# Attention in a hybrid trunk layer: the prompt's probabilities transposed by DMA instead of TensorE

## The chip, the cores and the metric

The kernel runs on one core of a Trainium2 chip. The metric is device time in microseconds of one execution. TensorE multiplies matrices and writes to PSUM; VectorE (DVE), ScalarE (ACT) and GpSimd (POOL) work on SBUF, and the first two also on PSUM; SyncE (SP) issues most transfers. Each engine, and each queue of transfers, works through its own instructions in a fixed order, and waits on semaphores where an instruction needs another engine's result.

## The reference

One layer serves 1024 prompt tokens and 8 sample requests of 16 tokens with the same weights. After a modulated norm one wide projection gives the attention's q, k, v and gate, the inputs of a state-space (SSD) branch, and two merge gates. The attention is banded: a chunk of 64 tokens sees itself and the 8 chunks before it, with a bias by distance.

```python
def attend(q, k, v, bias, mask):
    s = jnp.einsum('bqhd,bkhd->bhqk', q, k).astype(jnp.float32) * (ATT_HEAD_DIM ** -0.5) + bias[None].astype(jnp.float32)
    s = jnp.where(mask, s, -1e30)
    p = jax.nn.softmax(s, axis=-1).astype(v.dtype)
    return jnp.einsum('bhqk,bkhd->bqhd', p, v)

q = rms_norm(q.reshape(b, s, ATT_HEADS, ATT_HEAD_DIM), q_norm_g)
k = rms_norm(k.reshape(b, s, ATT_HEADS, ATT_HEAD_DIM), k_norm_g)
o_att, k_st, v_st = attn_fn(q, k, v)
att_branch = (o_att.reshape(b, s, ATT_WIDTH) * jax.nn.silu(z_att)) @ w_att_proj
```

There are 16 heads of 64. The SSD branch, the two projections back, the gates and the output projection follow; the outputs also hold the last k and v rows and the states. The change touches the attention alone. All values are float32.

## The kernel before, in words

Tokens: 1024 prompt and 128 sample tokens, 1152 (`NT`) in all, nine tiles of 128. A large product is made of three matmuls in a reduced float32 form, high part by high part, high by low and low by high, so weights and operands are split in two (L334, L335).

**Units.** The attention is done in eight units of two heads (`attention(u)`, L910). A unit has four parts, written as Python generators:

- `dense_gen` (L915): `dense_tok` (L487) makes q, k and v of the unit for nine token tiles, 24 matmuls a tile (L506 to L508), each into one of two PSUM banks "d"; after a tile `ev` (L923) copies q and k to the buffer `qk` (L926) with their squares (L928) on ACT and v on DVE (L929, L932). `dense` (L427; matmuls L442, L443, L445) then makes the next unit's gate columns z.
- `prelude` (L945): in three parts (first four tiles, next four, the sample tokens' tile) it norms q and k on POOL (L955 to L958), transposes them on TensorE (L980, for the sample tokens L990) and splits them into the operands `qh, ql, kh, kl` of the scores. There is one set of these; the set of unit u comes free when the last scores of unit u are done. Part one also takes places for the keys to be stored (`ko`) and the two heads' biases.
- `prompt` (L1037): the scores, softmax and weighing of the prompt, in six rounds.
- `sample` (L1141): the same for the sample requests against the cache, in two halves, with ten transposes of its own by the helper `transposed`.

**A prompt row block.** For query block m (128 tokens) a head has n = min(m,4)+1 blocks of 128 keys. The scores (L1101) go to PSUM; DVE adds the bias, negates and takes the row's least value (`negated`, L1024); ACT exponentiates with a row sum (`exps`, L1019), DVE scales by the reciprocal (L1020, L1021). The n blocks of probabilities are transposed on TensorE (`transposed`, L1031), copied from PSUM back into the same place by ACT (first four, L1033) and DVE (the fifth, L1035), and weighed with v on TensorE (`weigh`, L1054); DVE multiplies the result by the gate (L1106).

**Places.** Score rows lie in SBUF places "S" of 640 columns, nine of them; a place holds one head's row of a block. Blocks 0 and 3 share a pair of places, and 1 and 2. `ko` and the two biases also lie in "S" places.

**Rounds.** `ROUNDS` (L1065) lists, for each round, the score pieces, the blocks then weighed, and the blocks then transposed.

**What sets the order.** `run` (L841) plays a small planner. It steps the dense generator, adds the TensorE cost that each step yields to a clock, and gives the same times a ratio (0.95 here) as credit to "paced" generators (`prompt`, `sample`); "urgent" ones (`prelude`, stores) go first whenever they can. Waits are written as due times on that clock (`until`, `pause`), for instance:

```python
sfree[0] = clock[0] + 300 + sum(3.2 * x[2] for x in pieces)
tpt[m] = clock[0] + 1100
```

`sfree` is the time from which the next round, or the sample's scores, may use the score banks "s"; `tpt[m]` the time from which block m may be weighed. The order of the calls is the order that a scheduler below starts from: it may move an instruction forward where its operands are ready sooner, except for those under `late`, which stay behind the instruction before them on their engine. SP's queue carries the loads of weights (L312), of the cache (L1154, L1179) and of biases (L971, L1150), and the stores of k, v and the attention result (L1000, L937, L1013).

## Time and profile before

| | us |
|---|---|
| median of 3 runs (1954.15 to 1954.44) | 1954.2 |
| the profiled execution | 1954.12 |
| its span, first to last instruction | 1952.4 |
| TensorE busy | 1938.9 |
| DVE / ACT / POOL busy | 1163.5 / 775.9 / 328.1 |
| attention's transposes L1031, first and last start | 111.8 and 736.7 |

In the rows below a line number is a line of the kernel, "PE" is TensorE and "PEld" its weight loads. The page's first part gives each engine's busy time, share of the span and instructions; the chain of work follows the last instruction back to what released it. A row of a group has line, engine, operation, tile written and read, shapes, count, then busy us and the mean ns of one, then the idle time before it and what ended it. A window row has the stretch, its length, then busy time and count of each engine asked for (PE, PEld, DVE, ACT, POOL), the granted clock, the DMA engines' busy share and GB/s. A timeline row has start, duration, engine, line, operation, tiles, shapes and count. A matmul's duration overlaps the next one's, so the cost of one is the distance between starts.

### The profile page before, as it was taken

What the parts mean: (1) busy time and instruction counts of PE and PEld (TensorE: products, weight loads), DVE (VectorE), ACT (ScalarE), POOL (GpSimd) and SP (SyncE); (2) the same over time, 40 slices, a digit from 0 to 9 for tenths busy, and PEclk for the clock granted to TensorE, in tenths of its full rate; (3) what the DMA queues carried; (4) which work ended last, traced back from release to release, by engine and by line L of the source; (5) the groups of instructions that cost most, each with busy time, mean ns of one, the idle gap of its engine ahead of it and who ended that gap; (6) DMA issues with size and microseconds to landing.
All of it is one profiled execution on the core that took longest, in us unless ns stands there. A gap on an engine that the chain in (4) does not pass through costs nothing.

```text
span 1952.4 us, 34857 instructions
## 1 busy us (share of the span) xinstructions
PE 1938.9 (99%) x14041; PEld 1856.1 (95%) x14041; DVE 1163.5 (60%) x2409; ACT 775.9 (40%) x1579; POOL 328.1 (17%) x624
## 2 busy tenths in 40 slices
PE   8999999999999999999999999999999999999999
PEld 5989999899998899999999999999999999999999
DVE  7455545555455766666666766666674334777732
ACT  8444444444444565344434434345351301111200
POOL 0312223122221201211221221122212100000000
PEclk9999999999999999999999999999999999999999
DMA  9223343233332443334233333332337642331241
GB/s 374 63 70 122 103 138 118 72 119 109 131 111 71 133 125 119 129 117 131 92 127 119 116 105 106 117 118 91 118 119 292 232 140 92 105 104 56 86 143 53
DMA packets 81208, 238.61 MB, mean 122 GB/s; under 512 B 14284, under 2 KB 15320, under 8 KB 81048
## 3 DMA queue, kind: packets, MB, share of 16 engines
q1 hardware_dynamic: 72088, 207.74, 32.4%
q0 software_dynamic: 8960, 28.65, 3.8%
q8 instruction: 110, 1.80, 0.4%
q14 instruction: 50, 0.41, 0.1%
HBM read 192.70 MB, written 43.66 MB: 121 GB/s over the span
## 4 chain that ended last, share of the span: by engine, by line
PE 98%; ACT 0%; DVE 0%; DMA 0%; issue 0%; SPq 0%; DVEq 0%; ACTq 0%
PE d L442 14%; PE d L443 14%; PE d L445 14%; PE s L442 6%; PE s L445 6%; PE s L443 6%; PE d L508 5%; PE d L506 5%; PE d L507 5%; PE g L1031 3%; PE g L1054 3%; PE g L1542 2%; PE s L1101 2%; PE g L1515 1%; PE g L1562 1%; PE g L1101 1%
## 5 line engine op out<-in xcount | busy, mean ns | idle before, releaser
L442 PE MATMUL d<-rarena 128*128 128x384 f32 x1520 | 515.8, 339 | 0.0
L443 PE MATMUL d<-rarena 128*128 128x384 f32 x1520 | 511.3, 336 | 0.0
L445 PE MATMUL d<-rarena 128*128 128x384 f32 x1520 | 511.0, 336 | 0.0
L443 PEld LDWEIGHTS d<-rarena 128*128 128x128 f32 x1520 | 285.6, 188 | 2.8 <-issue 2.6
L442 PEld LDWEIGHTS d<-rarena 128*128 128x128 f32 x1520 | 285.7, 188 | 2.3 <-issue 0.9
L445 PEld LDWEIGHTS d<-rarena 128*128 128x128 f32 x1520 | 285.9, 188 | 0.4 <-issue 0.4
L334 ACT ACTIVATE rarena<-arena 128x1024 fp32r<-128x1024 f32 x92 | 97.4, 1059 | 330.9 <-PE s L443 238.3
L442 PE MATMUL s<-rarena 128*128 128x384 f32 x640 | 216.8, 339 | 0.0
L445 PE MATMUL s<-rarena 128*128 128x384 f32 x640 | 214.3, 335 | 0.0
L443 PE MATMUL s<-rarena 128*128 128x384 f32 x640 | 214.1, 334 | 0.0
L506 PE MATMUL d<-va_att,rarena 128*128 128x384 f32 (+1 forms) x559 | 194.1, 348 | 0.0
L508 PE MATMUL d<-va_att,rarena 128*128 128x384 f32 (+1 forms) x559 | 193.1, 345 | 0.0
L507 PE MATMUL d<-va_att,rarena 128*128 128x384 f32 (+1 forms) x559 | 190.2, 341 | 0.0
L335 DVE TENSOR_TENSOR rarena<-arena,rarena 128x1024 fp32r<-128x1024 f32 x92 | 113.2, 1231 | 81.8 <-ACT rarena L334 81.4
L1019 ACT ACTIVATE arena<-arena 128x640 f32<-128x640 f32 (+3 forms) x144 | 101.3, 706 | 70.6 <-DVE arena L1119 40.5
L442 PEld LDWEIGHTS s<-rarena 128*128 128x128 f32 x640 | 120.3, 188 | 1.1 <-issue 1.0
L443 PEld LDWEIGHTS s<-rarena 128*128 128x128 f32 x640 | 120.3, 188 | 0.0
L445 PEld LDWEIGHTS s<-rarena 128*128 128x128 f32 x640 | 120.2, 188 | 0.0
L1033 ACT ACTIVATE arena<-g 128x512 f32<-128x512 f32 (+3 forms) x144 | 71.3, 523 | 106.2 <-PE g L1031 106.0
L508 PEld LDWEIGHTS d<-va_att,rarena 128*128 128x128 f32 x559 | 105.2, 188 | 3.6 <-issue 3.2
L506 PEld LDWEIGHTS d<-va_att,rarena 128*128 128x128 f32 x559 | 105.6, 189 | 2.7 <-issue 1.9
L507 PEld LDWEIGHTS d<-va_att,rarena 128*128 128x128 f32 x559 | 105.3, 188 | 0.5 <-DVE arena L643 0.4
(345 smaller groups left out, 3224.1 us busy)
## 6 DMA issues: line engine op xcount, KB each, us to landing
arena<-in_wall_dram SPq DMA_DIRECT2D x85, 512.0 KB
arena<-in_kc_dram SPq DMA_DIRECT2D x64, 256.0 KB
arena<-in_vc_dram SPq DMA_DIRECT2D x64, 256.0 KB
arena<-acs_d SPq DMA_DIRECT2D x20, 576.0 KB
gate_d<-arena POOLq DMA_DIRECT2D x48, 192.0 KB, 2.8
arena<-y_d SPq DMA_DIRECT2D x15, 576.0 KB
arena<-in_wssd_dram SPq DMA_DIRECT2D x16, 512.0 KB
arena<-eacs_d SPq DMA_DIRECT2D x28, 288.0 KB
```

The lines of the kernel that those rows point to most:

```text
L334: keep(nc.scalar.activation(hi.r[:, c], b.ap, AF.Copy))
L335: keep(nc.vector.tensor_tensor(lo.r[:, c], b.ap, hi.ap[:, c], ALU.subtract))
L442: nc.tensor.matmul(ps, hi.r[:, wc], kh.r[:, tok], start=k == 0, stop=False)
L443: nc.tensor.matmul(ps, hi.r[:, wc], kl.r[:, tok], start=False, stop=False)
L445: nc.tensor.matmul(ps, lo.r[:, wc], kh.r[:, tok], start=False, stop=k == nk - 1)
L506: nc.tensor.matmul(ps, kh.r[:, tok], wh, start=j == 0, stop=False)
L507: nc.tensor.matmul(ps, kh.r[:, tok], wl, start=False, stop=False)
L508: nc.tensor.matmul(ps, kl.r[:, tok], wh, start=False, stop=j == KT - 1)
L1019: nc.scalar.activation(p, p, AF.Exp, bias=sm_[:, 4 + e:5 + e], scale=-1.0, accum_out=sm_[:, 6 + e:7 + e])
L1031: nc.tensor.transpose(ps[:, s * P:(s + 1) * P], p[:, (j + s) * P:(j + s + 1) * P], ident)
L1033: nc.scalar.activation(pt[:, j * P:(j + n) * P], ps[:, :n * P], AF.Copy)
L1054: late(nc.tensor.matmul(po[e * HD:e * HD + HD, a * P:(a + 1) * P], v.ap[:, vc:vc + HD], x.ap[:, o + i * P:o + (i + 1) * P], start=i == 0, ...
```

## The change

The prompt's probabilities are no longer transposed on TensorE. After the softmax, `turn(m)` runs for block m, as an urgent generator, for both heads:

1. It takes a second pair of places (`turned`), shared by blocks 0 and 3 and by 1 and 2 as before.
2. ACT copies the row from its place to the new one, taken as 16-bit words, so that all low halves of the float32 words come first and all high halves after (`words` to `planes`).
3. A transfer on SP's queue transposes the 2n blocks of 128x128 half-words from there back into the old place.
4. Due 7.5 us after the probabilities, ACT (head 1) and DVE (head 0) put the halves together again as words in the new place, from which `weigh` reads.
5. The old pair of places is freed then, and the block may be weighed 4.5 us later.

The third column of `ROUNDS` and the transposes in the round loop are gone; a round now also waits until its blocks have a due time, and takes places in pairs, only when no block still waits for its second pair. The due time of the score banks gets longer.

To make room for a tenth "S" place, `qk` has 16 blocks instead of 18, so that the ninth token tile lies where the first lay, and its eviction waits in `ev` until the first tokens are transposed; there is one "d" place (the sample's query block) instead of two and one "p" instead of two; the sample's own keys get a place "k" of their own, so that `ko` can be freed after its store; "t" has six places instead of five.

```diff
-    L_ATT = arena.set_layout(Z0, [("Q", 1, 18 * P), ("T", 5, NT), ("S", 9, 640), ("U", 2, 640), ("K", 4, 512), ("q", 1, 256), ("d", 2, 256),
-                                  ("p", 2, 128), ("n", 2, 36 + 3 * 16), ("t", 5, 14)])
+    L_ATT = arena.set_layout(Z0, [("Q", 1, 16 * P), ("T", 5, NT), ("S", 10, 640), ("U", 2, 640), ("K", 4, 512), ("q", 1, 256), ("d", 1, 256),
+                                  ("k", 1, 128), ("p", 1, 128), ("n", 2, 36 + 3 * 16), ("t", 6, 14)])
...
             def ev(t, ps):
-                c = qk.ap[:, 2 * t * P:2 * (t + 1) * P]
+                while t == 8 and "turned" not in st:
+                    blocked[0] = "q and k of the first tokens"
+                    yield None
+                c = qk.ap[:, 2 * (t % 8) * P:2 * (t % 8 + 1) * P]
...
+                    st["turned"] = True
                 else:
+                    ks = yield from walloc(lay, "k", P)
+                    qd = yield from walloc(lay, "d", 256)
+                    late(nc.gpsimd.memset(qd.ap, 0.0))
+                    yield from pause(600)
...
                     nc.scalar.activation(ko.ap[:, 512:], ps[:, P:], AF.Copy, scale=par["qk_g"][:, 1:2])
+                    nc.scalar.activation(ks.ap, ps[:, P:], AF.Copy, scale=par["qk_g"][:, 1:2])
                     yield 218
                     yield from pause(900)
                     dma(h["out_k"][u], ko.ap)
+                    stored(ko)
...
+            pairs = {0: 3, 1: 2, 2: 1, 3: 0}
+            def planes(x, at, n):
+                return x.ap[:, at:at + n * P].bitcast(U16).rearrange("p (t k) -> p t k", t=2)
+            def words(x, at, n):
+                return x.ap[:, at:at + n * P].bitcast(U16).rearrange("p (k t) -> p t k", t=2)
+            def turn(m):
+                n = min(m, 4) + 1
+                if pairs.get(m) in claimed:
+                    yield from ready(lambda: m in turned)
+                else:
+                    claimed.add(m)
+                    t = yield from wpair(lay, "S", 640)
+                    for q, at in ((m, place[m][0][1]), (pairs.get(m), {0: 4 * P, 2: 2 * P}.get(pairs.get(m), 0))):
+                        if q is not None:
+                            turned[q] = [(b, at) for b in t]
+                turning[0] -= 1
+                for e in range(2):
+                    yield from until(probs[m] + 800 * e)
+                    (x, at), (y, _) = place[m][e], turned[m][e]
+                    nc.scalar.activation(planes(y, at, n), words(x, at, n), AF.Copy)
+                    dma(x.ap[:, at:at + n * P].bitcast(U16).rearrange("p (i k) -> p i k", k=P),
+                        y.ap[:, at:at + n * P].bitcast(U16), transpose=True)
+                for e in range(2):
+                    yield from until(probs[m] + 800 * e + 7500)
+                    (x, at), (y, _) = place[m][e], turned[m][e]
+                    if e:
+                        nc.scalar.activation(words(y, at, n), planes(x, at, n), AF.Copy)
+                    else:
+                        nc.vector.tensor_copy(words(y, at, n), planes(x, at, n))
+                xs = place.pop(m)
+                if pairs.get(m) not in place:
+                    for x, _ in xs:
+                        x.free()
+                tpt[m] = clock[0] + 4500
...
             ROUNDS = (
-                (((0, 0, 128, 0, 0), (1, 0, 256, 0, 128), (2, 0, 384, 1, 0)), (), ()),
-                (((3, 0, 512, 0, 0), (4, 0, 512, 1, 0)), (), (0, 1, 2)),
-                (((4, 512, 128, 0, 0), (5, 0, 320, 0, 128), (5, 320, 320, 1, 0)), (0, 1, 2), (3,)),
-                (((6, 0, 320, 0, 0), (6, 320, 320, 1, 0)), (3,), (4, 5)),
-                (((7, 0, 320, 0, 0), (7, 320, 320, 1, 0)), (4, 5), (6, 7)),
-                ((), (6, 7), ()),
+                (((0, 0, 128, 0, 0), (1, 0, 256, 0, 128), (2, 0, 384, 1, 0)), ()),
+                (((3, 0, 512, 0, 0), (4, 0, 512, 1, 0)), ()),
+                (((4, 512, 128, 0, 0), (5, 0, 320, 0, 128), (5, 320, 320, 1, 0)), (0, 1, 2)),
+                (((6, 0, 320, 0, 0), (6, 320, 320, 1, 0)), (3,)),
+                (((7, 0, 320, 0, 0), (7, 320, 320, 1, 0)), (4, 5)),
+                ((), (6, 7)),
             )
...
-                        if m in (2, 3):
-                            place[m] = [(x, at) for x, _ in place[3 - m]]
-                        else:
-                            place[m] = []
-                            for e in range(2):
-                                place[m].append(((yield from walloc(lay, "S", 640)), at))
+                        t = yield from wpair(lay, "S", 640, lambda: turning[0] == 0)
+                        for q in {m, pairs.get(m, m)}:
+                            place[q] = [(x, {0: 4 * P, 2: 2 * P}.get(q, 0)) for x in t]
...
+                        turning[0] += 1
+                        urgent.append(turn(m))
...
-                sfree[0] = clock[0] + 300 + sum(3.2 * x[2] for x in pieces)
-                for m in ts:
-                    n = min(m, 4) + 1
-                    yield from until(sfree[0])
-                    for e in range(2):
-                        yield from until(probs[m] + 700 * e)
-                        x, at = place[m][e]
-                        transposed(x.ap[:, at:at + n * P], x.ap[:, at:at + n * P], n)
-                        yield 109 * n
-                    tpt[m] = clock[0] + 1100
-                    sfree[0] = max(sfree[0], clock[0] + 1500)
+                sfree[0] = clock[0] + 1000 + sum(4.4 * x[2] for x in pieces)
```

More of the change, by code (lines that the diff above doesn't have):

```diff
@@ L266, in walloc, with wpair @@
                 yield None
+    def wpair(lay, tag, cols, cond=lambda: True):
+        while True:
+            try:
+                if cond():
+                    a = alloc(lay, tag, cols)
+                    try:
+                        return [a, alloc(lay, tag, cols)]
+                    except NoSlot:
+                        a.free()
+                        raise
+                blocked[0] = "places for what is transposed"
+            except NoSlot as x:
+                blocked[0] = str(x)
+            yield None
     x0_ = Z0
@@ L1057, in weigh @@
                 for j in js:
-                    for x, _ in place.pop(j):
-                        if not any(x is y for q in place.values() for y, _ in q):
+                    for x, _ in turned.pop(j):
+                        if pairs.get(j) not in turned:
                             x.free()
@@ L1065, in prompt @@
             ROUNDS = (
[6 rows of a table removed]
-            )
-            for pieces, js, ts in ROUNDS:
[6 rows of a table added]
+            )
+            for pieces, js in ROUNDS:
+                yield from ready(lambda: all(j in tpt for j in js))
                 yield from until(max([sfree[0]] + [tpt[j] for j in js]))
```

34 lines of the change are left out of this document (18 added, 16 removed).

## The prediction, made before the changed kernel was run

> **What bounds the kernel now.** I read the page's busy shares first, then the chain that ended last, then the windows of one attention unit, then that unit's timeline engine by engine. From the page:
>
> ```profile
> PE 1938.9 (99%) x14041; PEld 1856.1 (95%) x14041; DVE 1163.5 (60%) x2409; ACT 775.9 (40%) x1579; POOL 328.1 (17%) x624
> PE 98%; ACT 0%; DVE 0%; DMA 0%; issue 0%; SPq 0%; DVEq 0%; ACTq 0%
> ```
>
> TensorE is the path: 98% of the chain. Work taken off it shortens the run unless a new wait opens on it. The groups and the chain by line price the work that goes:
>
> ```profile
> L1031 PE MATMUL g<-arena x560: 270/272/329, 111.8 to 736.7; 128*128 128x128 f32 x187
> by line: PE d L442 13.7%; PE d L443 13.6%; PE d L445 13.6%; PE s L442 5.7%; PE s L445 5.7%; PE s L443 5.7%; PE d L508 5.3%; PE d L506 5.2%; PE d L507 5.1%; PE g L1031 3.4%; PE g L1054 3.1%; PE g L1542 1.8%; PE s L1101 1.7%; PE g L1515 1.5%;
> 122.15 1.20 PE g L1031 x11
> 486.80 1.09 PE g L1031 x10
> ```
>
> The 270 ns are overlapped; on the chain eleven transposes take 1.20 us, ten 1.09: 109 ns each. With the gaps where TensorE changes its kind of work, L1031 holds 3.4% of 1952.4 = 66.4 us for 560, 118.5 ns each.
>
> The windows of three units, with DVE and ACT busy as fourth and fifth figures and the DMA share next to last, and the same window for ACT's evictions L1033:
>
> ```profile
> 343.20:423.80 80.60, 80.60 (x684) 73.81 (x683) 44.40 (x139) 37.73 (x89) 19.89 (x37) 1.00 0.34 111
> 423.80:504.40 80.60, 80.60 (x684) 73.80 (x683) 44.48 (x139) 37.61 (x89) 19.90 (x37) 1.00 0.33 110
> 504.40:585.00 80.60, 80.60 (x684) 73.81 (x683) 45.53 (x141) 37.78 (x91) 19.90 (x37) 1.00 0.33 108
> 423.80:504.40 80.60, 8.96 (x18) 1.00 0.33 110
> ```
>
> A unit takes 80.6 us, TensorE is never idle in it, ACT is busy 37.6 us and DVE 44.5, the DMA engines a third; the granted clock is 1.00, so no clock gain or loss enters.
>
> **Transposes removed.** Row block m (128 query tokens) has min(m,4)+1 blocks of 128x128 per head, 1+2+3+4+4x5 = 30, so 60 per unit and 480 in all; the other 80 of the 560 belong to the sample requests (2 halves x 5 x 8) and stay. Bounds: 480 x 109 ns = 52.3 us, 480 x 118.5 = 56.9. Some gaps stay because the weighing still interrupts the dense stream, so I take 54, 6.75 a unit.
>
> **Copies added.** Durations of the same engines on other widths:
>
> ```profile
> L334 ACT ACTIVATE rarena<-arena 128x1024 fp32r<-128x1024 f32 x92 | 97.4, 1059 | 330.9 <-PE s L443 238.3 <-issue 44.1 <-PE g L443 41.6
> L1019 ACT ACTIVATE arena<-arena 128x640 f32<-128x640 f32 x80 | 65.9, 825 | 40.6 <-DVE arena L1119 40.5
> L1033 ACT ACTIVATE arena<-g 128x512 f32<-128x512 f32 x96 | 56.5, 596 | 93.5 <-PE g L1031 93.3
> L1019 ACT ACTIVATE arena<-arena 128x512 f32<-128x512 f32 x16 | 11.4, 716 | 12.9 <-DVE arena L1024 12.9
> L1021 DVE TENSOR_SCALAR arena<-arena 128x640 f32<-128x640 f32 x80 | 54.3, 678 | 2.5
> L1035 DVE COPY arena<-g 128x128 f32<-128x128 f32 x80 | 23.0, 287 | 23.5 <-PE g L1031 22.8
> ```
>
> ACT: (825-716)/128 = 0.85 ns per element and 0.28 us fixed; a block row of five is 1280 half-words, 1.37 us (1.28 from the 1024-wide row). Per unit 16 copies into planes (15360 elements) and 8 back into words (7680): 23040 x 0.85 + 24 x 0.28 = 26.3 us; out go the prompt's evictions, 8.96 less the sample's 2 x 0.6 = 7.8; the second copy of the sample's keys adds 0.4. ACT: 37.6 to 56.5 us of a unit of 74, 76%. DVE: 8 copies, 7680 x 678/640 = 8.1 us, against 8 x 0.287 = 2.3 removed: 44.5 to 50.3, 68%. Half-words at a stride of two stand in no row; were they twice as dear, ACT would hold 76 us of 74 and bind. I take the row's rate, as those copies too are one element per step. Both engines then have room on average: cost 0 on the path, with the cover being the two "d" banks (one 24-matmul bank, 24 x 0.17 = 4.2 us, of grace for each eviction).
>
> **Transposing transfers added.** 128 a program: 16 a unit on SP's queue, 480 blocks x 64 KB = 31.5 MB. No row shows one. Nearest rows:
>
> ```profile
> q1 hardware_dynamic: 72088, 207.74, 32.4%
> gate_d<-arena POOLq DMA_DIRECT2D x48, 192.0 KB, 2.8
> y_d<-arena POOLq DMA_DIRECT2D x11, 576.0 KB, 3.2
> SPq L312 <- DVE rarena L335: 468.2, 72, 18.1
> SPq L1179 <- PE s L1167: 218.1, 15, 17.8
> ```
>
> Lower bound, by bytes: q1 moves 207.74 MB in 32.4% of 1952.4 us, so 31.5 MB take 96 us of the engines, 12 a unit. Upper bound, by packets: 0.324 x 16 x 1952.4 / 72088 = 140 ns of one engine each; a packet per 256-byte row is 122880 rows, 1075 us of all 16, 134 a unit: more than a unit. I take the byte end, as a row of 256 bytes should not cost what a mean packet of 2.9 KB does; then the DMA share rises from 0.33 to about 0.5 and one lands in some 3 us, like plain ones of 192 to 576 KB. That stays hidden. The Trainium skill ("Advanced Engine Details and Errata", X-Bar Transpose) says as much, transposing transfers about as fast as regular ones; "DMA: Bandwidth & Descriptors" (Latency and other measured facts) gives 261 GB/s with a split middle dimension, by which the 31.5 MB would be an estimated 121 us and the sum the same.
>
> SP is in order: behind a transfer that waits for its plane copy stand weight, cache and bias loads. The rows show SP already waiting 18 us at a stretch for a free buffer without a stall of TensorE, so that cover is large; a transposing transfer behind such a load would be late by as much, which counts among the rivals.
>
> **The chain of one unit.** The saving is had only if prompt rounds R0 to R5 and the next prelude fit into 74 us. Their places in the old unit:
>
> ```profile
> 425.10 0.33 PE L1101 MATMUL s<-rarena 64*128 64x128 f32 x2
> 473.86 2.40 PE L1054 MATMUL g<-arena 128*64 128x128 f32 x40
> 481.20 1.03 PE L980 MATMUL g<-arena 128*128 128x128 f32 x8
> 492.93 2.40 PE L1054 MATMUL g<-arena 128*64 128x128 f32 x40
> 504.33 0.38 PE L990 MATMUL g<-arena 128*128 128x128 f32 x2
> 482.10 0.20 POOL L955 TENSOR_SCALAR arena<-arena 128x16 f32<-128x16 f32 x1 [24.55 <-DVE arena L932]
> 495.34 0.61 POOL L958 TENSOR_TENSOR arena<-arena 128x256 f32<-128x256 f32 x1
> ```
>
> R0 starts at 425.1, R4 (weighing blocks 4 and 5) 48.8 later, the next unit's first q/k transposes at +56.1, R5 at +67.8, the sample tokens' transposes L990 at +79.2.
>
> New, in the code's own due times: R0 at 0. The probabilities of block 2 are due at 5.6, its copies back 7.5 and 8.3 later, so pair (1,2) comes free at 13.9. Only then is there a place for block 4: besides the two biases there are eight places, four pairs, and all are taken. R1 starts at 13.9 (old rule: 4), R2 at 20.8. Block 3's pair is free at 26.9, block 4 takes it and gives up its own at 33.2, where R3's scores start; R4 needs block 5 weighable, 40.5. In the old due times R4 comes at 33.3, and the trace has 48.8: 15.5 of lag from the sample's steps and from the credit that paces prompt work. In the new waits the credit refills, so I take about half, 7: R4 at 47.5. From R4 on: 3.6 for its own work, 2.1, 11.6 and 5.3 for the three parts of the prelude, 0.6 for the later clearing of the sample's query block, 1.9 to the next R0: 25.1, so 72.6 us. TensorE's work is 80.6 - 6.75 = 73.9. They are as good as equal, the due times are generous (copy 1.4, transfer 3, copy 1.4, against 12.8 from probabilities to weighing), so TensorE stays the bound.
>
> The wait of the ninth token tile for the first tokens' transposes: dense work before it is nine tiles (9 x 4.2 = 37.4 us) with R0 to R4 (1.2 + 1.4 + 2.5 + 2.3 + 3.6 = 11 by the code's costs) and 5 of the sample part's 7, 54 us after the start, when those transposes are due at 51; behind it stand the next gate columns (12.5 us) and they cover the rest of the prelude. Cost 0 with that cover, 8 us a unit (POOL's two norms, 482.1 to 496.0, less what runs beside them) if it were gone. Single k and d places: the sample part must end before the prelude's third part; R5 and sample end today some 9 us before it; 0.
>
> **What stays as new stall.** Bounded below by nothing less than 0 (less waiting at L1031 could even add a gain of its 9.2 us), above by the whole saving. The nearest row is the waiting that such weighing meets today:
>
> ```profile
> L1054 PEld LDWEIGHTS g<-arena 128*64 128x64 f32 x960 | 53.4, 137 | 9.5 <-issue 7.0 <-PE g L1191 1.6 <-ACT arena L1019 0.5
> ```
>
> I take as much again, 9.5. Sum against the profiled execution (1954.12 us, its span 1952.4): 1954.1 - 54 + 9.5 = 1909.6. The median, 1954.2, is the same within 0.1.
>
> **Rivals.**
> (a) Places bind; slower. If the old lag of 15.5 us stays whole the cycle is 81; and since R1, R3 and R4 each hang on a turn before them, each microsecond that a turn (copy, transfer, copy) takes over its 8.3 adds up to three. It decides from a cycle of 80.6. With turns 3 us longer than due: 81 + 9 = 90, 9.4 x 7 cycles = +66: 2020; with 1 us, 81 + 3 = 84 and 1978. For it: at four pairs nothing overlaps between rounds 0 and 1. Against: the due times hold margin.
> (b) In-order queues. ACT and DVE carry copies that wait for a transfer; what stands behind is the evictions of the dense banks. Eight such waits per engine and unit, each over the grace of 4.2 us by 1 us, give back 64: 1954.1 - 54 + 64 = 1964. For it: ACT at 76%. Against: the grace.
> (c) Half the saving is lost the same way, 0.5 us a wait: 1932.
> (d) The transfers bind. At the packet bound, 134 us plus today's 27 a unit: 161 instead of 80.6, 1954 + 8 x 80 = 2600. The Trainium skill speaks for it: "VectorE: DVE Perf Modes" (The three transpose paths) gives 1309 ns for one 128x128 block by DMA; its estimate one after another is 120 x 1.309 = 157 us a unit. No row here shows either; the same rows that land 576 KB in 3.2 us speak against.
>
> **How the numbers follow.** Forecast 0.45; (c) 0.06; (b) 0.14, centred a little above the old time; (a) 0.28; (d) 0.07. Within 0.2% (3.9 us, about what a measurement of this kernel can tell from no change) falls 0.04, out of (b); faster is 0.45 + 0.06 + 0.02 of (b) = 0.53; slower the other 0.43. The range goes from all gaps gone and no stall, 1954.1 - 56.9 - a few = 1892, to 1990 in the middle of (a): left out are (d), some 0.09 of (a) and 0.03 below. The forecast's own range is 1895 to 1930.
>
> **What would show it.** Right: L1031 down to 80, ACT near 56 us a unit, units of 74 to 76 us with TensorE still 98% or more, transposing transfers landing in 3 to 4 us. Wrong: TensorE idle before L1054 or L1101 with DMA, ACT or DVE as releaser (a), before dense matmuls with ACT as releaser (b), units above 80 us, or a DMA share near 0.9 (d).

## The result, and the profile after

The changed kernel takes 1965.2 us (median, 1961.6 to 1968.7), the one before 1954.2. The ratio is 1.0056 (95% interval 1.0037 to 1.0076): slower by 11 us, where 44 us faster was forecast. The profiled execution took 1968.7 us with a span of 1966.9.

First the page's busy shares and the chain that ended last, of the changed kernel:

```profile
PE 1910.4 (97%) x13561; PEld 1814.8 (92%) x13561; DVE 1171.7 (60%) x2411; ACT 902.4 (46%) x1653; POOL 326.3 (17%) x624
PE 78%; DMA 9%; ACT 6%; DVE 4%; issue 3%; SPq 1%; POOL 0%; ACTq 0%; DVEq 0%
```

The transposes are gone (13561 matmuls, 480 fewer), and TensorE is busy 28.5 us less. But its idle time, span less busy, went from 1952.4 - 1938.9 = 13.5 us to 56.5. The chain says where to look: 78% TensorE in place of 98%, and 9% DMA and 6% ACT in place of nothing.

Then the windows of two attention units, with columns as in the prediction (length, busy time of PE, PEld, DVE, ACT, POOL, granted clock, DMA share, GB/s):

```profile
430.60:514.60 84.00, 77.58 (x624) 69.14 (x622) 46.03 (x139) 53.27 (x98) 20.60 (x37) 0.98 0.62 152
514.60:600.10 85.50, 77.36 (x625) 69.11 (x623) 45.31 (x141) 53.77 (x100) 18.99 (x38) 0.98 0.64 151
```

A unit was to shrink from 80.6 us to about 74; it takes 84.0 and 85.5, with TensorE idle 6.4 and 8.1 us in it. The DMA engines' share went from 0.33 to 0.63, and the granted clock is no longer 1.00.

The waits of the changed kernel (engine, tile, line, what it waited for: us in total, times, longest) name the place. L1104 and L1106 are the two copies that put the halves together again; L948 to L951 are the evictions of the dense banks "d":

```profile
ACT arena L1104 <- DMA arena<-arena: 140.5, 46, 9.0
DVE arena L1106 <- DMA arena<-arena: 78.3, 52, 4.7
```

```profile
PE d L459 <- DVE arena L951: 9.2, 5, 2.1
PE s L1221 <- DVE arena L1053: 7.2, 6, 1.4
PE d L523 <- DVE arena L951: 7.2, 6, 1.7
PE g L1258 <- ACT arena L1254: 5.1, 4, 1.7
PE g L1122 <- ACT arena L1104: 3.3, 3, 1.9
```

46 of ACT's 64 copies and 52 of DVE's 64 find their transfer not landed and wait for it, ACT up to 9.0 us. The last five rows are TensorE's largest waits inside the attention. Only 9.2 + 7.2 = 16.4 us of them are before dense matmuls, whose banks DVE had not emptied (L951); 7.2 are before the sample tokens' scores, whose bank "s" was still being read (L1053), 5.1 before the transpose of the sample tokens' result (L1258, after ACT's L1254), and 3.3 before the weighing, for ACT's copy itself. One unit in the timeline: first SP's issues, then ACT and DVE, then every wait of TensorE between 430.6 and 514.6 us (a timeline row is start, duration, engine, line; a bracket holds the idle time before it and what ended it):

```profile
454.59 1.24 SPq L1098 DMA_TRANSPOSE arena<-arena  x1
455.93 0.53 SPq L329 DMA_DIRECT2D arena<-in_wall_dram  x1
456.54 1.81 SPq L1211 DMA_DIRECT2D arena<-in_kc_dram  x4
458.44 1.47 SPq L1098 DMA_TRANSPOSE arena<-arena  x1
```

```profile
453.51 2.00 ACT L1097 ACTIVATE arena<-arena 128x1024 uint16<-128x1024 uint16 x2
464.60 1.35 ACT L1104 ACTIVATE arena<-arena 128x1024 uint16<-128x1024 uint16 x1 [8.38 <-DMA arena<-arena]
465.82 0.80 ACT L1048 ACTIVATE arena<-arena 128x640 f32<-128x640 f32 x1
466.75 0.17 DVE L1049 RECIPROCAL arena<-arena 128x1 f32<-128x1 f32 x1 [6.49 <-ACT arena L1048]
493.34 1.63 ACT L1104 ACTIVATE arena<-arena 128x1280 uint16<-128x1280 uint16 x1 [2.10 <-DMA arena<-arena]
```

```profile
466.00 1.09 PE L1122 MATMUL g<-arena 128*64 128x128 f32 x14 [1.15 <-ACT arena L1104]
469.19 1.06 PE L1221 MATMUL s<-arena 128*32 128x512 f32 x8 [1.20 <-DVE arena L1053]
476.25 0.41 PE L1166 MATMUL s<-rarena 64*128 64x320 f32 x2 [0.71 <-DVE arena L1053]
479.94 0.44 PE L523 MATMUL d<-va_att,rarena 128*128 128x384 f32 x1 [1.64 <-DVE arena L951]
495.14 0.33 PE L1258 MATMUL g<-arena 128*128 128x128 f32 x1 [1.73 <-ACT arena L1254]
```

ACT has taken block 3's second head into planes by 455.5. SP issues a weight load and four cache loads first; the transposing transfer of that head goes out at 458.4 and has landed at 464.6. ACT stands still for 8.4 us before L1104. TensorE loses 1.15 us waiting for that copy before it can weigh block 3. Behind the copy in ACT's order are exponentials (L1048, 465.8); DVE waits 6.49 us for them and then reads the score bank late (L1053), which costs the sample tokens' scores another 1.20 us. The five waits add up to 6.43 us, the 6.4 that TensorE is idle in this unit, and only the 1.64 us at 479.9 are for a dense bank. The last wait shows that a short delay is enough: ACT waits only 2.10 us for a transfer at 493.3, the copy behind it (L1254) is late, and TensorE loses 1.73 us.

The copies by themselves are close to what was said of them. First the view of line L1098 (issue durations on SP's queue, then the landing), then the queue that carries the transfers, then the widest copies by form:

```profile
L1098 SPq DMA_TRANSPOSE arena<-arena x128: 1174/1310/2544, 105.4 to 749.7; - x128
DMA to landing us min/median/max: 2.7/3.0/6.1
```

```profile
q1 hardware_dynamic: 199064, 239.22, 42.0%
```

```profile
L1097 ACT ACTIVATE arena<-arena 128x1280 uint16<-128x1280 uint16 x64 | 80.4, 1264 | 11.4 <-DVE arena L1050 11.2
L1104 ACT ACTIVATE arena<-arena 128x1280 uint16<-128x1280 uint16 x32 | 53.1, 1659 | 53.3 <-DMA arena<-arena 53.3
L1106 DVE COPY arena<-arena 128x1280 uint16<-128x1280 uint16 x32 | 29.7, 928 | 41.7 <-DMA arena<-arena 41.7
```

The profile has the landing of only 8 of the 128 transfers; their median is 3.0 us, as forecast. For the 98 that a copy waited for, the time from issue to landing can be read from the copy's start: 2.3 to 7.1 us, with a median of 3.8.

### The profile page after: what moved, and what is told of

It reads as the page before. It is cut to its first block, busy times and chain, and to the rows that moved or that the text cites. A ratio compares the mean times of both kernels' runs of the same rounds, so it can differ in the third digit from the quotient of the medians.

```text
span 1966.9 us, 34369 instructions
## 1 busy us (share of the span) xinstructions
PE 1910.4 (97%) x13561; PEld 1814.8 (92%) x13561; DVE 1171.7 (60%) x2411; ACT 902.4 (46%) x1653; POOL 326.3 (17%) x624
## 3 DMA queue, kind: packets, MB, share of 16 engines
q1 hardware_dynamic: 199064, 239.22, 42.0%
## 4 chain that ended last, share of the span: by engine, by line
PE 78%; DMA 9%; ACT 6%; DVE 4%; issue 3%; SPq 1%; POOL 0%; ACTq 0%; DVEq 0%
PE d L459 13%; PE d L460 13%; PE d L462 13%; DMA arena<-arena 7%; PE s L459 6%; PE s L462 6%; PE s L460 6%; PE d L523 3%; PE d L524 2%; PE d L525 2%; ACT arena L1048 2%; ACT arena L1097 2%; PE g L1599 2%; PE g L1572 1%; PE g L1122 1%
## 5 line engine op out<-in xcount | busy, mean ns | idle before, releaser
L459 PEld LDWEIGHTS d<-rarena 128*128 128x128 f32 x1528 | 289.1, 189 | 17.4 <-issue 12.1
L460 PEld LDWEIGHTS d<-rarena 128*128 128x128 f32 x1528 | 288.9, 189 | 2.9 <-issue 2.8
L462 PEld LDWEIGHTS d<-rarena 128*128 128x128 f32 x1528 | 288.7, 189 | 2.5 <-DVE rarena L425 1.3
L459 PE MATMUL s<-rarena 128*128 128x384 f32 x632 | 214.4, 339 | 0.0
L460 PE MATMUL s<-rarena 128*128 128x384 f32 x632 | 211.5, 335 | 0.0
L462 PE MATMUL s<-rarena 128*128 128x384 f32 x632 | 211.5, 335 | 0.0
L352 DVE TENSOR_TENSOR rarena<-arena,rarena 128x1024 fp32r<-128x1024 f32 x91 | 111.7, 1227 | 75.6 <-ACT rarena L351 75.2
L1104 ACT ACTIVATE arena<-arena 128x1280 uint16<-128x1280 uint16 (+2 forms) x64 | 82.9, 1296 | 140.6 <-DMA arena<-arena 140.5
L1097 ACT ACTIVATE arena<-arena 128x1280 uint16<-128x1280 uint16 (+4 forms) x128 | 126.1, 998 | 18.1 <-DVE arena L1050 16.5
L459 PEld LDWEIGHTS s<-rarena 128*128 128x128 f32 x632 | 118.8, 188 | 1.7 <-issue 1.6
L460 PEld LDWEIGHTS s<-rarena 128*128 128x128 f32 x632 | 118.8, 188 | 0.0
L462 PEld LDWEIGHTS s<-rarena 128*128 128x128 f32 x632 | 118.7, 188 | 0.0
```

What stands on the lines that cost most here:

```text
L352: keep(nc.vector.tensor_tensor(lo.r[:, c], b.ap, hi.ap[:, c], ALU.subtract))
L459: nc.tensor.matmul(ps, hi.r[:, wc], kh.r[:, tok], start=k == 0, stop=False)
L460: nc.tensor.matmul(ps, hi.r[:, wc], kl.r[:, tok], start=False, stop=False)
L462: nc.tensor.matmul(ps, lo.r[:, wc], kh.r[:, tok], start=False, stop=k == nk - 1)
L1097: nc.scalar.activation(planes(y, at, n), words(x, at, n), AF.Copy)
L1104: nc.scalar.activation(words(y, at, n), planes(x, at, n), AF.Copy)
```

## The experiments

Three theories were set against one another. **L**: transfers that land late stop ACT and DVE, whose order is fixed, and with them what stands behind, the evictions above all (rival (b)); its two forms are that the transfer is late because of SP's order, or because it shares the DMA engines with other loads. **P**: the chain through the score places sets the unit (rival (a)). **C**: the copies' own time. Each run was timed beside the kernel before on the same chip, which took 1954.1 to 1954.3 us in all of them.

### The transfers taken out, the transposes taken out, the order alone

Without the transfers: the transposing call is dropped, and the copies back read the place that the plane copy read.

```diff
-                    dma(x.ap[...], y.ap[...], transpose=True)
...
-    nc.scalar.activation(words(y, at, n), planes(x, at, n), AF.Copy)
+    nc.scalar.activation(words(y, at, n), words(x, at, n), AF.Copy)
```

> The changed kernel without the transposing transfers; the copies into planes and back stay (the copy back reads the untouched words, so the attention weighs with probabilities that are not transposed: that part of the computation is left out). Theory L (late landing: ACT and DVE stand at the copies back until a transfer has landed, and the evictions behind them hold TensorE up): the stalls go, units of 74 to 76 us, 1900 to 1915. Theory P (places: four pairs make the rounds follow each other so slowly that the unit is 81 to 85 us whatever the transfer takes, since the due times stay): within 5 us of the changed kernel, 1960 to 1970. Theory C (the copies' own time on ACT): half of the loss stays, 1930 to 1950.

The kernel before without the prompt's transposes and their evictions:

```diff
-                        transposed(x.ap[:, at:at + n * P], x.ap[:, at:at + n * P], n)
-                        yield 109 * n
```

> The kernel before with the prompt's 480 transposes and their evictions left out (probabilities not transposed), order and due times else as before: the ceiling of what can be gained. All theories: 1954 - 52 to 57 = 1897 to 1902. Above 1920 the price of a transpose was taken too high.

The changed kernel with its places, due times and rounds, but with TensorE's transposes in place of the copies and the transfer:

```diff
-                    nc.scalar.activation(planes(y, at, n), words(x, at, n), AF.Copy)
-                    dma(...)
...
+                    transposed(x.ap[:, at:at + n * P], y.ap[:, at:at + n * P], n)
+                    yield 109 * n
```

> The changed kernel with its places, waits and due times, but the transposes on TensorE again, from the first pair of places to the second at the time at which the copies back stood; no copies, no transfers. Theory L: the new structure costs little, TensorE's work is the old one, 1954 to 1962. Theory P: the chain of rounds is still 81 to 85 us a unit and TensorE's work no longer its filler alone, 1965 to 1985.

| | us | ratio to before (95%) |
|---|---|---|
| without the transfers | 1913.3 | 0.979 (0.976 to 0.982) |
| before, without transposes | 1907.5 | 0.976 (0.973 to 0.979) |
| transposes in the new order | 1961.5 | 1.0037 (1.0023 to 1.0051) |

These make a ladder. Taking the transposes out of the old kernel is worth 1954.3 - 1907.5 = 46.8 us, evictions included: 97 ns a transpose, the most that the change can bring in that order of work, and less than the 52 to 57 expected. The new order with all of its copies costs 1913.3 - 1907.5 = 5.8 us, and the new order without them 7.1 us (1961.5 - 1954.3): the copies' own time is nothing that shows (C is out), and the rearranged places and waits cost some 6 us. The transfers then cost 1965.2 - 1913.3 = 51.9 us. TensorE's busy time in the kernel before without transposes (span 1904.8), then the page of the run without transfers, and one of its units:

```profile
PE 1886.2 (99%) x13561; PEld 1806.4 (95%) x13561; DVE 1157.1 (61%) x2345; ACT 718.4 (38%) x1451; POOL 323.4 (17%) x624
PE 1892.3 (99%) x13561; PEld 1805.0 (94%) x13561; DVE 1175.0 (61%) x2411; ACT 901.6 (47%) x1653; POOL 332.8 (17%) x624
329.00:404.60 75.60, 74.78 (x624) 67.42 (x623) 46.12 (x139) 52.98 (x99) 20.39 (x37) 1.00 0.37 118
```

With ACT just as busy (52.98 us) the unit takes 75.6 us, close to the forecast 74. The spans differ by 1966.9 - 1911.8 = 55.1 us: 56.5 - 19.5 = 37.0 of TensorE's idle time and 18.1 of longer busy time for the same 13561 matmuls, of which the granted clock (0.995 against 1.000) is 1966.9 x 0.005 = 9.8. The other 8.3 us of longer busy time were not traced.

### The waiting copies put on POOL

```diff
-                    if e:
-                        nc.scalar.activation(words(y, at, n), planes(x, at, n), AF.Copy)
-                    else:
-                        nc.vector.tensor_copy(words(y, at, n), planes(x, at, n))
+                    nc.gpsimd.tensor_copy(words(y, at, n), planes(x, at, n))
```

> The changed kernel with both copies back on GpSimd, which has nothing of the dense stream behind them. Theory L: ACT and DVE no longer stand for a transfer, most of the stalls of the evictions go: 1915 to 1940. Theory P: the same as the changed kernel or worse, 1960 to 1980. Theory C: a third of ACT's added copies goes, 1945 to 1960.

1981.9 us, ratio 1.0139 (1.0109 to 1.0168): slower still, and above the ranges of all three theories. From its waits (L1103 is the copy on POOL, L816 the eviction of the gate columns):

```profile
POOL arena L1103 <- DMA arena<-arena: 243.3, 72, 13.2
ACT arena L1048 <- POOL arena L1103: 13.8, 4, 5.8
PE d L459 <- DVE arena L816: 20.5, 4, 6.2
```

The wait moved with the copies. POOL now stands up to 13.2 us, and its copy of a row of five blocks takes 1.76 us. ACT's exponentials wait for POOL in turn, and TensorE for the evictions of L816, up to 6.2 us; how the copies on POOL make L816 late was not followed. That an idle engine takes the wait is not enough, then; the likely reason, not shown, is that others depend on what stands behind it there too.

### Who holds the transfer: SP's order or the DMA engines

Biases and cache loads of the sample requests moved from SP's queue to POOL's:

```diff
-                    dma(kc.ap, h["kc"][u, 4 * bg + i])
+                    store(kc.ap, h["kc"][u, 4 * bg + i])
```

> The changed kernel with the sample's cache and bias loads (18 a unit) issued by GpSimd instead of SP, so that no transposing transfer stands behind them on SP's queue; what the DMA engines carry is the same. Theory L1 (the transfers are late because SP issues them late, behind loads): most of the 52 us that the transfer costs comes back, 1915 to 1935, and the waits of the copies back for a transfer fall from 219 us to under 100. Theory L2 (they are late because the 16 DMA engines are shared with those loads): 1955 to 1970, waits over 180.

2005.9 us, ratio 1.026 (1.023 to 1.029), above both ranges; the waits of the copies rose to 290 us. With the cache loads off SP's queue, the same kind of wait in its timeline (SP, then ACT):

```profile
379.19 1.32 SPq L1098 DMA_TRANSPOSE arena<-arena  x1
380.61 0.53 SPq L329 DMA_DIRECT2D arena<-in_wall_dram  x1
381.26 2.00 SPq L1098 DMA_TRANSPOSE arena<-arena  x1
```

```profile
378.12 1.99 ACT L1097 ACTIVATE arena<-arena 128x1024 uint16<-128x1024 uint16 x2
390.38 1.35 ACT L1104 ACTIVATE arena<-arena 128x1024 uint16<-128x1024 uint16 x1 [8.25 <-DMA arena<-arena]
```

SP issues the transfer at 381.3, 1.2 us after its plane copy ended (2.9 us in the stall shown above), and it has landed at 390.4, after 9.1 us instead of 6.1. The 16 DMA engines are full meanwhile (a share of 1.12 from 382 to 385 us and 1.46 from 385 to 388; above 1, packets overlap in the records). So SP's order alone does not make it late: out of the loads' way on SP it lands later still, beside a weight load and the cache loads that POOL issues at that time. Why 9.1 and not 6.1 is not settled.

The trace of the changed kernel divides the delay. Its six longest waits on ACT, 7.1 to 9.0 us in six of the eight units, are all of the form shown above: SP issues the transfer 2.9 to 3.8 us after its plane copy ended, behind four cache loads, and it lands 5.7 to 6.3 us after its issue, against the median of 3.0. SP's order and the time on the DMA engines beside the loads so account for about 3 us each. With the loads on POOL's queue the first part shrinks and the second grows: in its five longest waits on ACT, 1.0 to 1.7 us and 7.2 to 9.9 us.

### One cache load in place of four

```diff
-                for i in range(4):
-                    kc = yield from walloc(lay, "K", 512)
-                    dma(kc.ap, h["kc"][u, 4 * bg + i])
-                    kcs.append(kc)
+                kc = yield from walloc(lay, "K", 512)
+                dma(kc.ap, h["kc"][u, 4 * bg])
+                kcs = [kc] * 4
```

and the same for the values. In the changed kernel, and then in the kernel before as a control:

> The changed kernel, with one cache load in place of four for the sample tokens' keys and one for their values in each half of a unit: the four requests of a half all use the first one's cache, so the sample tokens' attention is not computed as in the reference. 6 MB of loads less stand beside the transposing transfers of a unit's prompt tokens, and 12 issues less on SP; matmuls and copies are the same. If the loads that share the 16 DMA engines are what makes the transfers land late (3.0 us as a rule, 6.1 and more beside the loads), the 219 us of ACT and DVE waiting for transfers falls below 110, TensorE's idle time from 56 us below 35, and the time to 1920 to 1945 us. If the places or the fixed order alone set the 84 us unit, the time stays within 1955 to 1970.

> The kernel before the change, with a quarter of the cache loads (the four requests of a half use the first one's cache, so the sample tokens' attention is not computed as in the reference). It has no transposing transfers for the loads to stand beside. If the 30 us that the same edit gave the changed kernel came through the transfers, this stays within 1950 to 1956. If the loads cost either kernel that much by themselves, it comes to 1920 to 1940, and the late landing of the transfers explains less.

The changed kernel comes to 1934.8 us, ratio 0.990 (0.987 to 0.993); the one before stays at 1954.4, ratio 1.0001 (0.9990 to 1.0013). So 30.4 of the 51.9 us that the transfers cost come of their meeting the cache loads, on SP's queue or on the DMA engines, and the loads cost nothing where there are no transposing transfers. The waits of the changed kernel with a quarter of the loads:

```profile
DVE arena L1106 <- DMA arena<-arena: 88.7, 50, 4.3
ACT arena L1104 <- DMA arena<-arena: 83.0, 44, 4.8
```

Two expectations missed: TensorE's idle time is 37.4 us, not below 35, and the waits for transfers are 171.7 us, not below 110. DVE's rose from 78 to 89, ACT's fell by 57 us, its longest from 9.0 to 4.8. The six waits of over 7 us are gone, and with them most of TensorE's waits for the score banks. The other 21.5 us that the transfers cost stay, and no run here isolates their cause.

### The same loads at other places of SP's queue

```diff
                     dma(kc.ap, h["kc"][u, 4 * bg + i])
+                    yield from pause(2000)
```

and the same behind each load of values, in the changed kernel.

> The changed kernel, whole computation, with 2 us between one cache load and the next in place of four issued in a burst. If the burst on the 16 DMA engines is what makes the transfers land late, the waits of ACT and DVE for transfers fall from 219 to under 150 us and the time to 1935 to 1955. If the bytes count and not the burst, the waits stay near 219 and the time within 1955 to 1970; if the later loads hold up the sample tokens' products on TensorE, it is above 1970.

1945.0 us, ratio 0.996 (0.994 to 0.998), 20 us better with the whole computation, and 0.4% faster than before the change. ACT waits 80.9 us, longest 4.7, and DVE 76.2: together 157, just above the 150 expected. The edit did not spread the loads, though: its timeline shows the four still issued as one burst.

```profile
375.01 1.97 SPq L1211 DMA_DIRECT2D arena<-in_kc_dram  x4
```

What changed is where the burst stands. In SP's rows from 100 to 760 us the changed kernel has 21 places where transposing transfers follow a burst of cache loads within 1 us, and this one 2; the others follow 1.3 us later or more. Bytes and bursts are equal, so neither costs by itself; what differs is where the burst stands to the transfers. The sample tokens' steps moved with it, however: TensorE's waits before their scores and before the transpose of their result, 7.2 and 5.1 us in the changed kernel, are 0.6 here. How much of the 20 us is due to each was not separated, and whether really spread loads would do better was not tried.

### Later copies, more places

The rest of the loss could be the due times or the places. Four runs of the changed kernel changed the due time of the copies back (7.5 us after the probabilities), three with ten places:

```diff
-                    yield from until(probs[m] + 800 * e + 7500)
+                    yield from until(probs[m] + 800 * e + 10500)
```

> The changed kernel with the copies back due 10.5 us after the probabilities instead of 7.5 (weighing still 4.5 us after them), so that they stand later in ACT's and DVE's order. Theory L (engines stand waiting for landings): the waits shrink by up to 3 us each, 1920 to 1945. Theory P (places): every turn is 3 us longer, three of them hang on each other in a unit, the cycle grows by 6 to 9 us, 1975 to 2010.

With 9.5 us there and 2.5 instead of 4.5 us from the copies to the weighing:

> The copies back due 2 us later (9.5), weighing 2 us sooner after them (2.5), so that the time from probabilities to weighing stays and only places are held longer. Theory L: 1930 to 1955, with some of the wait moved to TensorE before the weighing. Theory P: 1965 to 1985.

With 9.5 us, and the loads on POOL's queue:

> Cache and bias loads on GpSimd's queue and the copies back due 9.5 us after the probabilities. Theory L with either cause: the best of the four, 1910 to 1930, below the kernel before. Theory P: above 1960.

And with a quarter of the loads, so that the room of three cache places gives two more score places, at 7.5 and at 10.5 us:

```diff
-    ("S", 10, 640), ("U", 2, 640), ("K", 4, 512)
+    ("S", 12, 640), ("U", 2, 640), ("K", 1, 512)
```

> As the run with a quarter of the cache loads (same part of the computation changed), and with the room of three of the four cache places given to two more score places: twelve in place of ten. If the chain through the places binds beside the late transfers, it is at least 10 us faster than its sibling with ten places; if only the late transfers bind, it is within 5 us of it.

> As the run with twelve places (same part of the computation changed), and the copies back due 10.5 us after the probabilities in place of 7.5. With ten places and all loads the later time cost 26 us, although the copies waited less. If it was the places that made it dear, it costs nothing here, the waits of ACT and DVE for transfers fall below 40 us, and the time is that of twelve places or up to 20 us less, near 1915. If later copies are dear by themselves (the order of the rounds waits for them), it loses 10 us or more here too.

| places, cache loads | copies back due | us | ACT and DVE waiting for transfers |
|---|---|---|---|
| 10, all | 7.5 | 1965.2 | 140.5 + 78.3 |
| 10, all | 9.5 (weighing 2.5 after) | 1972.3 | 116.4 + 95.6 |
| 10, all | 10.5 | 1991.3 | 59.7 + 107.6 |
| 10, all, on POOL's queue | 7.5 | 2005.9 | 147.3 + 142.9 |
| 10, all, on POOL's queue | 9.5 | 1985.5 | 111.2 + 107.9 |
| 10, a quarter | 7.5 | 1934.8 | 83.0 + 88.7 |
| 12, a quarter | 7.5 | 1931.2 | 60.9 + 60.7 |
| 12, a quarter | 10.5 | 1943.9 | 57.9 + 49.8 |

Ratios to before, for the rows that were not given yet: 1.009 (1.006 to 1.012), 1.019 (1.016 to 1.022), 1.016 (1.009 to 1.023), 0.988 (0.985 to 0.991) and 0.995 (0.993 to 0.997). The queue change on POOL at 9.5 us had runs of 1980 and 1991 and says little more than that.

All three runs with ten places and a later due time came out in the range of P and not in that of L. Waiting on purpose is no cure: 3 us of later due time took 81 us of ACT's waiting away, added 29 of DVE's, and cost 26 us. There TensorE waits most before the weighing, in the waits of the run due at 10.5 us, for ACT's copy and for DVE, whose reciprocal L1049 stands right behind its copy:

```profile
PE g L1122 <- ACT arena L1104: 11.6, 5, 2.4
PE g L1122 <- DVE arena L1049: 10.7, 5, 2.6
```

With a quarter of the loads two more places are worth 3.6 us, within the 5 that were put as the bound for places that do not bind; so at 7.5 us and with few loads the places are not what costs. With all loads there was no room for twelve. The later due time costs 12.7 us with twelve places and a quarter of the loads, against 26 with ten places and all loads. Places and loads both differ between the two, so what part of a longer turn goes through the places stays open; P is neither shown nor ruled out where a turn gets longer. The waits with twelve places and the later time are 107.7 us, not below 40 as was expected of P.

### One head by transfer, the other on TensorE

```diff
-                    t = yield from wpair(lay, "S", 640)
+                    t = yield from walloc(lay, "S", 640)
...
+                yield from until(probs[m] + 1500)
+                transposed(z0, z0, n)
+                yield 109 * n
+                yield from until(probs[m] + 8300)
+                nc.vector.tensor_copy(words(y, at, n), planes(x, at, n))
```

(z0 is the first head's row, transposed in place; the second head goes by planes and transfer, and only DVE puts it together again.)

> The changed kernel with the transfer for the second head of each block only; the first head is transposed on TensorE in its own place, as before the change (240 transposes and their evictions are back). It needs three score places a block in place of four, half the transfers and half the copies; the copies back are on VectorE. The saving left is 240 times 97 ns, 23 us, against which stand up to 6 us of order and copies. If late landing and places cost by the transfer, half of the 52 us is lost: 1954 - 23 + 6 + 26, about 1963. If the loss falls faster than by half (no second transfer queued behind the first, room in the places), it is 1935 to 1950, faster than before the change.

1937.3 us, ratio 0.991 (0.989 to 0.994): faster than both kernels, with the whole computation, and within the better of the two expected ranges. Its page and its wait for transfers (L1105 is the copy on DVE):

```profile
PE 1919.2 (99%) x13801; PEld 1830.1 (95%) x13801; DVE 1181.8 (61%) x2443; ACT 805.9 (42%) x1589; POOL 315.2 (16%) x624
PE 96%; DVE 1%; ACT 1%; DMA 1%; issue 0%; SPq 0%; ACTq 0%; DVEq 0%
DVE arena L1105 <- DMA arena<-arena: 74.8, 43, 6.5
```

The time is that of the saving and the order alone: 1954.2 - 23.3 (240 transposes at 97 ns) + 6 = 1937. By this sum the transfers cost nothing any more. DVE still waits for 43 of 64, up to 6.5 us, but ACT never does, TensorE is 96% of the chain, and its idle time is 1934.4 - 1919.2 = 15.2 us. Half the transfers, copies back on DVE alone and three places a block instead of four came together here; which of them made the loss go was not separated. With 2 us between the cache loads in the code as well:

> The kernel that transposes by transfer for the second head alone (1937 us), with the same 2 us between cache loads. Its TensorE idles 15 us, near the 13.5 of the kernel before, so that at most some 3 us are to be had: 1932 to 1938. If spreading delays the sample tokens' products, it is above 1940.

1939.5 us, ratio 0.993 (0.991 to 0.995): no gain, just above the expected range, as TensorE's idle time had left little to win back.

## Why the prediction was wrong, step by step

**The step that failed** is the one on the transposing transfers: "one lands in some 3 us ... That stays hidden", and with it "cost 0 on the path, with the cover being the two "d" banks". The transfer was costed alone, and the cover was taken for more than it is. Behind the cache loads a transfer is issued some 3 us late and lands after 5.7 to 6.3 us more; ACT's copy then waits 7.1 to 9.0 us. And the two dense banks do not cover what else stands behind a waiting copy: the score banks, the sample tokens' transpose and the weighing itself. In the unit shown 4.79 of TensorE's 6.43 us of waiting are there and 1.64 before a dense matmul, and a wait of 2.10 us on ACT, half of the grace of 4.2, cost TensorE 1.73 us. The transfers cost 51.9 us in all; 30.4 of them are shown to come of the cache loads.

Rival (b), the in-order queues, stood at 1964 with a chance of 0.14; the time came out at 1965. It had the right kind of wait, but that the number fits is in part luck: its picture was dense banks and eight waits a unit, each 1 us over the grace, and it had no loss of clock, which the prediction put at nothing and which took 9.8 us.

**Transposes removed**: forecast 54 us, measured at most 46.8 of time. The price of the work was right: without the transposes TensorE is busy 1938.9 - 1886.2 = 52.7 us less, 110 ns each, against the 109 read from the chain. But its idle time rose from 13.5 to 1904.8 - 1886.2 = 18.6 us, so that 97 ns each came back.

**Copies**: ACT was to have 56.5 us of a unit, it has 53.3; DVE 50.3, it has 46. For a row of five blocks 1.37 us were forecast on ACT; the plane copies take 1.26, the copies back 1.66. On DVE, by the forecast's rate, 1.36; measured 0.93. Their own time costs nothing, as forecast.

**Transfers, by bytes or by packets**: neither end. q1 has 199064 - 72088 = 126976 packets more, the 122880 rows of 256 bytes and 32 more a transfer, so the packets were counted right. Their price is between the bounds: a unit with transfers holds the engines 0.62 x 84.0 = 52.1 us, without them 0.37 x 75.6 = 28.0, so 24 us a unit, twice the 12 by bytes and far from 134. The share of 0.63 against the forecast 0.5 left less room beside the loads. Rival (d) is out, with 24 us a unit against its 134: a whole row of up to ten 16-bit blocks lands in 2.3 to 7.1 us. The Trainium skill ("VectorE: DVE Perf Modes", The three transpose paths) gives 1309 ns for one block, which made its estimate of 157 us a unit; the trace does not agree with adding it up block by block. The Trainium skill's 261 GB/s ("DMA: Bandwidth & Descriptors", Latency and other measured facts) is nearer, but 31.5 MB in 8 x 24 us is 164 GB/s here, counted as busy share.

**The chain of a unit**: R1 was to start 13.9 us after R0. The timeline of a unit has 14.0:

```profile
431.99 0.33 PE L1166 MATMUL s<-rarena 64*128 64x128 f32 x2
445.98 0.49 PE L1166 MATMUL s<-rarena 64*128 64x512 f32 x2
```

R2 starts 25.0 us after R0, with the transfers and without, where 20.8 was forecast. R4 starts 46.8 us after R0 in the run without the transfers (47.5 forecast) and 57.9 in the changed kernel. Without the transfers the unit takes 75.6 us, against 72.6 for the chain and 73.9 for TensorE's work. So this part was near for turns as short as forecast. How much of the loss goes through the places of rival (a), once late transfers make the turns longer, is not shown.

**New stall**: 9.5 us forecast; without the transfers it is 19.5 - 13.5 = 6.0. With them it is 43.0. The term was sized by the waits of a kernel in which no ACT or DVE copy waits for such a transfer.

## What to carry to other kernels

A transfer that an in-order engine waits for has to be costed beside the loads that can meet it, in the queue that issues it and on the DMA engines, and not by its median alone. Then list everything that stands behind the waiting copy on its engine, and for each item what the bound engine needs of it: here the dense banks had a grace of 4.2 us, but the scores, the sample tokens' transpose and the weighing made up most of TensorE's waiting in the unit shown. Doing half the transposes by transfer, with DVE alone waiting for them, kept half of the saving, less the 6 us of the new order. And a due time in the program's order was no substitute for a transfer that lands early: waiting 3 us longer on purpose took ACT's waits away and still made the kernel 26 us slower.

## What the runs showed of the hardware

A short stall of TensorE can cost more than its length. Windows of 1 us of the changed kernel, TensorE alone (length, busy, granted clock, DMA share, GB/s):

```profile
493.00:494.00 1.00, 0.41 (x6) 1.00 1.08 213
494.00:495.00 1.00, 0.00 (x0) 1.00 0.91 274
495.00:496.00 1.00, 0.86 (x4) 0.68 1.03 373
496.00:497.00 1.00, 1.00 (x5) 0.50 1.01 385
497.00:498.00 1.00, 1.00 (x5) 0.50 1.00 361
498.00:499.00 1.00, 1.00 (x8) 0.61 1.06 410
```

After 0.59 + 1.00 + 0.14 = 1.73 us of idle time the clock is at half for some 3.4 us, so that the stall costs 1.7 us more (0.32 + 0.50 + 0.50 + 0.39). Windows of 4 us from 100 to 752 us show six such dips of 1.7 us, 10.2 in all, about the 9.8 us of lost clock. Not every stall of that length brings one: after 2.04 us of idle time the clock stayed at 1.00 (the window has all engines before the clock).

```profile
335.56 0.41 PE L459 MATMUL d<-rarena 128*128 128x384 f32 x1 [2.04 <-DVE arena L951]
336.00:340.00 4.00, 4.00 (x25) 3.75 (x26) 0.74 (x2) 2.95 (x5) 3.14 (x12) 1.00 1.24 205
```

The Trainium skill ("TensorE: Matmul & The Clock Gate", Part 1) has the half clock come after an idle window of about 3.4 us and the full clock after a busy one of about 3.4 us. The length of the slow stretch agrees, but here an idle time of half a window was enough in one case and not in another.

A transposing transfer holds SP's queue 1.2 to 2.5 us at its issue (the row of L1098 above), against 0.3 to 0.8 for a weight load of 512 KB: 16 a unit at 1.31 us are 21 us of SP's time. And the copy that writes 16-bit halves at a stride of two costs ACT 1.66 us and DVE 0.93 for the same 1280 elements a partition (the rows of L1104 and L1106), and POOL 1.76.
